# The gate and up projections of an FFN by seven block products in place of eight

## The chip, the cores and the metric

One core of a Trainium2 chip runs the whole program: one inference step of a model with two layers that share one code path. The metric is the device time of a launch in microseconds. Three runs of the kernel before gave a median of 1646.72 us (1646.56 to 1646.89).

## The reference

There are 640 tokens (512 of a sample, 128 of a prompt), a width of 1024 and two layers. Each layer has a token mixer and a gated FFN; the change lies in the FFN and in what surrounds it:

```
h = rms_norm(x, p["g_pre_ffn"]) * (1.0 + scale2) + shift2
f = (jax.nn.silu(h @ p["w_gate"]) * (h @ p["w_up"])) @ p["w_down"]
x = x + gate2 * rms_norm(f, p["g_post_ffn"])
```

h is 640 x 1024, w_gate and w_up are 1024 x 2816, w_down is 2816 x 1024, all in float32. The vectors scale2, shift2 and gate2, and three more for the mixer, come from a modulation: m = silu(cond) @ w_mod + b_mod, per layer, for two conditions.

## The kernel before

**Precision.** A float32 matrix product is made of three matmuls in the fp32r format. Each operand is split into hi (a rounded copy) and lo (what is left). `split` lets ScalarE write hi (L125) and VectorE or GpSimd write lo as source minus hi (L121); `mm3` issues hi*hi, hi*lo and lo*hi into one PSUM bank (L187 to L189).

**Weights.** `chunk` loads 512 KB by SP's DMA queue (L172) into a slot "raw" (three slots of 128 x 1024) and splits it into two pairs "wh", "wl" of 128 x 512 (eight slots each). In a gate or up chunk the eight k tiles of one f tile (128 of the 2816 columns) lie side by side.

**Input.** Normed tokens lie transposed in hTh and hTl: eight k tiles, 640 token columns, of which token tile t owns columns 128 t to 128 t + 127; tile 4 is the prompt. For each token tile the tail of the mixer makes the output projection, its post-norm (L382, L385), the statistic for the next norm (L344, with the root on POOL, L136), the normed rows (L352), their transposes on TensorE (L355), the modulation by scale and shift (L365 on ScalarE, L367 on VectorE), and a split into hTh and hTl. Tile 4 comes last.

**The FFN.** There are 22 f tiles in groups of 8, 8 and 6. For an f tile, gate and up are computed over two halves of the tokens, columns 0 to 255 (tiles 0 and 1) and 256 to 639: per half and matrix 8 k tiles times three matmuls. Then ScalarE takes tanh (L983), VectorE two steps that make silu(gate) * up (L984, L985), and a split makes hi and lo of the slot ft. In the first group the first four half products are of tiles 0 and 1 of f tiles 0 and 1, so that they need not wait for tiles 2 to 4. Behind each group stands its part of w_down, accumulated in SBUF (L1020, L1022). With the last group the post-norm follows, the residual rows xt are loaded, and in layer 0 the norm and transposes for layer 1.

**Background.** While the FFN of layer 0 runs, the modulation of layer 1 is computed by steps between f tiles: 512 KB of w_mod per DMA (L299) into slots of their own (tiles qa, kt and ka), multiplied by four matmuls side by side in the columns of TensorE (L302).

**Order.** The program is traced as one stream, and a scheduler places each engine's instructions in a queue; the engines then go through their queues in order and wait for each other on semaphores. Eight PSUM banks are in use: two tiles "s" of two banks, two "pt" of one, "o" and "g" of one.

## Time and profile before

| | value |
|---|---|
| median of three runs | 1646.72 us |
| span of the profiled execution | 1647.5 us |
| PE busy | 1588.7 us, 96% |
| PEld busy | 1362.7 us, 83% |
| DVE busy | 803.2 us, 49% |
| ACT busy | 662.9 us, 40% |
| POOL busy | 389.3 us, 24% |
| HBM read | 167.17 MB |

PE is TensorE's matmul pipe, PEld its weight loads, which run beside it; DVE is VectorE, ACT is ScalarE, POOL is GpSimd, SP issues the DMAs. Busy time is a sum over the span, so an engine that is busy for half of it may still be late in one stretch. The FFN of layer 0 lies between about 355 and 811 us and more, that of layer 1 from about 1163 us to the end. The page gives no time of the execution but its span, which is therefore the profiled execution's own time.

### The profile page before, as it was taken

The page shows a single profiled execution, that of the slowest core. Times are in us where ns is not written, and L with a number is a line of the kernel's source. Part 1 is how long each engine was busy: PE and PEld are TensorE (multiplying, and loading weights), DVE is VectorE, ACT ScalarE, POOL GpSimd, SP SyncE. Part 2 cuts the span into 40 slices and gives each one's busy share as a digit, 9 for nine tenths or more (in the row PEclk, how much of TensorE's full clock was granted, in tenths as well). Part 3 has the DMA queues.
Part 4 walks back from the last instruction along what each step waited for, and adds up shares of the span by engine and source line. Part 5 has one row for each costly group of instructions (what it writes and reads, how often), then busy time and mean ns, then how long its engine had stood idle before and what let it go on. Part 6 is the DMA issues. An engine that isn't in the chain of part 4 may idle for free.

```text
span 1647.5 us, 24545 instructions
## 1 busy us (share of the span) xinstructions
PE 1588.7 (96%) x9643; PEld 1362.7 (83%) x9643; DVE 803.2 (49%) x1553; ACT 662.9 (40%) x1472; POOL 389.3 (24%) x338
## 2 busy tenths in 40 slices
PE   7999989999999999999999999998899999999998
PEld 5676767678987989889978877776799889988996
DVE  4557777683231223332376687767723222333335
ACT  5343676563222322222254447765523222212222
POOL 3124214552100211021041242254511021101102
PEclk9999999999999999999999999999999999999999
DMA  9854020255453253122242111102422222213212
GB/s 327 307 179 162 29 84 27 78 185 203 165 205 115 90 192 125 56 97 77 71 164 91 55 61 55 39 26 103 167 90 77 71 84 77 68 49 102 77 65 77
DMA packets 62900, 180.08 MB, mean 109 GB/s; under 512 B 9520, under 2 KB 20784, under 8 KB 62784
## 3 DMA queue, kind: packets, MB, share of 16 engines
q1 hardware_dynamic: 62784, 178.50, 32.1%
q8 instruction: 76, 1.25, 0.3%
q14 instruction: 40, 0.33, 0.1%
HBM read 167.17 MB, written 11.30 MB: 108 GB/s over the span
## 4 chain that ended last, share of the span: by engine, by line
PE 83%; DVE 5%; issue 4%; ACT 4%; POOL 3%; DMA 1%; SPq 0%; DVEq 0%; POOLq 0%; ACTq 0%
PE s L187 8%; PE s L188 8%; PE s L189 8%; PE g L187 6%; PE g L189 6%; PE g L188 6%; PE o L187 5%; PE o L188 5%; PE o L189 5%; PE pt L187 5%; PE pt L188 4%; PE pt L189 4%; PE s L302 2%; PE o L602 2%; PE pt L593 2%
## 5 line engine op out<-in xcount | busy, mean ns | idle before, releaser
L121 DVE TENSOR_TENSOR wl<-raw,wh 128x512 fp32r<-128x512 f32 x240 | 189.0, 795 | 351.3 <-ACT wh L125 348.4
L125 ACT ACTIVATE wh<-raw 128x512 fp32r<-128x512 f32 x344 | 212.1, 631 | 342.9 <-PE s L188 153.6
L121 POOL TENSOR_TENSOR wl<-raw,wh 128x512 fp32r<-128x512 f32 x120 | 164.8, 1379 | 719.4 <-ACT wh L125 717.6
L187 PE MATMUL s<-hTh,wh 128*128 128x384 f32 (+1 forms) x928 | 290.0, 313 | 0.0
L188 PE MATMUL s<-hTl,wh 128*128 128x384 f32 (+1 forms) x928 | 289.0, 311 | 0.0
L189 PE MATMUL s<-hTh,wl 128*128 128x384 f32 (+1 forms) x928 | 288.3, 311 | 0.0
L187 PEld LDWEIGHTS s<-hTh,wh 128*128 128x128 f32 x928 | 174.4, 188 | 6.1 <-ACT P L983 4.2
L189 PEld LDWEIGHTS s<-hTh,wl 128*128 128x128 f32 x928 | 174.6, 188 | 0.0
L188 PEld LDWEIGHTS s<-hTl,wh 128*128 128x128 f32 x928 | 174.2, 188 | 0.2
L187 PE MATMUL pt<-hTh,wh 128*128 128x384 f32 (+1 forms) x448 | 140.1, 313 | 4.0 <-ACT hTh L125 3.9
L188 PE MATMUL pt<-hTl,wh 128*128 128x384 f32 (+1 forms) x448 | 139.6, 312 | 0.0
L189 PE MATMUL pt<-hTh,wl 128*128 128x384 f32 (+1 forms) x448 | 138.8, 310 | 0.0
L187 PE MATMUL g<-wh,hTh 128*128 128x512 f32 x256 | 106.5, 416 | 0.6 <-ACT hTh L125 0.5
L188 PE MATMUL g<-wl,hTh 128*128 128x512 f32 x256 | 103.8, 405 | 0.0
L189 PE MATMUL g<-wh,hTl 128*128 128x512 f32 x256 | 103.3, 404 | 0.4 <-DVE hTl L121 0.4
L136 POOL TENSOR_TENSOR rs<-rs,mhalf 128x1 f32<-128x1 f32 (+3 forms) x66 | 58.2, 885 | 176.8 <-DVE rs L133 126.9
L187 PEld LDWEIGHTS pt<-hTh,wh 128*128 128x128 f32 x448 | 84.5, 189 | 7.7 <-ACT hTh L125 5.1
L547 DVE TENSOR_REDUCE nm<-s 128x1 f32<-128x640 f32 x96 | 77.5, 820 | 27.0 <-PE s L546 13.9
L548 ACT ACTIVATE P<-s,nm 128x640 f32<-128x640 f32 x96 | 76.3, 797 | 28.8 <-DVE nm L547 27.4
L189 PEld LDWEIGHTS pt<-hTh,wl 128*128 128x128 f32 x448 | 84.8, 189 | 0.0
L188 PEld LDWEIGHTS pt<-hTl,wh 128*128 128x128 f32 x448 | 84.4, 188 | 0.3 <-DVE hTl L121 0.3
L984 DVE SCALAR_TENSOR_TENSOR P<-P,s 128x384 f32<-128x384 f32 (+1 forms) x58 | 28.2, 486 | 101.2 <-ACT P L983 101.2
(370 smaller groups left out, 3177.9 us busy)
## 6 DMA issues: line engine op xcount, KB each, us to landing
raw<-in_w_gate SPq DMA_DIRECT2D x44, 512.0 KB
raw<-in_w_up SPq DMA_DIRECT2D x44, 512.0 KB
raw<-in_w_down SPq DMA_DIRECT2D x44, 512.0 KB
kt<-in_w_mod SPq DMA_DIRECT2D x40, 512.0 KB
raw<-in_w_in SPq DMA_DIRECT2D x32, 512.0 KB
ka<-in_w_mod SPq DMA_DIRECT2D x24, 512.0 KB
raw<-in_w_out SPq DMA_DIRECT2D x16, 512.0 KB
qa<-in_w_mod SPq DMA_DIRECT2D x16, 512.0 KB
```

Of the source, the lines that this page charges most:

```text
L121: eng.tensor_tensor(lo, src, hi.bitcast(F32), op=ALU.subtract)
L125: self.S.activation(hi, src, AF.Copy)
L136: self.G.tensor_tensor(out, out, self.mhalf[:, :out.shape[-1]], op=ALU.pow)
L187: self.T.matmul(out, ah, bh, start=first, stop=False)
L188: self.T.matmul(out, ah, bl, start=False, stop=False)
L189: self.T.matmul(out, al, bh, start=False, stop=last)
L302: self.T.matmul(p[32 * j:32 * j + 32, 0:w], self.c2[:, c:c + 32], raw[k][j // 2][:, j % 2 * w:(j % 2 + 1) * w], start=c == 0, stop=c == 2 ...
L547: V.tensor_reduce(nm[:, s:s + 1], sc[:, :, :320], axis=AX.XY, op=ALU.max, negate=True)
L548: S.activation(P[s].rearrange("p (a b) -> p a b", a=2), sc[:, :, :320], AF.Exp, bias=nm[:, s:s + 1], accum_out=sm[:, s:s + 1])
L593: T.transpose(p[:, j - j0, i * 128:(i + 1) * 128], P[:, j * 128:(j + 1) * 128], self.ident)
L602: T.matmul(o[64 * i:64 * i + 64, 0:128], vt[:, j if nkt == 5 else 5], PT[:, j, i * 128:(i + 1) * 128], start=j == 0, stop=j == nkt - 1)
L984: V.scalar_tensor_tensor(ta, ta, 1.0, gp, op0=ALU.add, op1=ALU.mult)
```

## The change

The 640 x 1024 input is cut into 2 x 2 blocks: tokens 0 to 319 and 320 to 639 (so token tile 2 is cut in two), k tiles 0 to 3 and 4 to 7. The weights of a pair of f tiles are cut in the same way, 512 x 128 each. The eight block products of such a pair become seven, by Winograd's form of Strassen's algorithm: four input blocks enter as they are or combined with others, and so do the weight blocks; the results are formed by additions.

`combine` makes the combined inputs, 64 columns at a time, five times per layer, from the normed and modulated rows m in float32; those of columns c and c + 320 enter one call, so the first three calls need token tiles 2 and 3, the last two also tile 4. Products 6, 7 and 3 read new operands, product 5 reads a combination put in place into hTh and hTl, products 1, 2 and 4 read plain blocks. `wunit` makes four differences of a unit's weight blocks (a unit is gate or up of one pair, so there are 44 in all) and splits seven pieces. `fproduct` is one product, 12 matmuls of 320 columns; `funit` has the seven with five additions from PSUM on VectorE. For four units (the first two pairs) products 1 and 2 are placed early, between the combinations, and their weights are loaded a second time for the rest. Groups are now 2, 3, 3 and 3 pairs, the next group's first gate unit stands before w_down, the modulation of layer 1 goes through the "s" slots in 256 KB pieces (`mod_s`), and the last rows xt through "raw". In the trace of after, the split stands at L119, mm3 at L185, the products at L1035 to L1037, the combinations at L983 to L988, weight differences at L1014.

```diff
-HALVES = [(0, 256), (256, 384)]
-GROUPS = [list(range(0, 8)), list(range(8, 16)), list(range(16, 22))]
+HT = TOK // 2
+GROUPS = [[0, 1], [2, 3, 4], [5, 6, 7], [8, 9, 10]]
...
+    def mod_s(self, l, pair, p, bank):
+        src = self.a["w_mod"][l].rearrange("(k p) (i n) -> p k i n", p=128, n=D)
+        for k in range(KT):
+            for j in range(4):
+                raw = self.s()
+                self.SY.dma_start(raw, src[:, k, pair[j // 2], j % 2 * 512:(j % 2 + 1) * 512])
+                self.T.matmul(p[32 * j:32 * j + 32], self.c2[:, 2 * k:2 * k + 32], raw, start=k == 0, stop=k == KT - 1)
+            yield
+        self.mod_finish(l, pair, 512, 0, p, lambda what: self.s(), bank)
...
+        sl = slice(t * 128, min((t + 1) * 128, stop))
+        n = sl.stop - sl.start
+        if n > 0:
+            self.split(self.hTh[:, 4 * i:4 * i + 4, sl], self.hTl[:, 4 * i:4 * i + 4, sl], ht[:, :, 0:n], eng)
...
+    def operands(self):
+        s2, s3 = (self.tl(self.pa, [128, 2, 4, HT], "kt", 2, F32R) for _ in range(2))
+        s4 = [self.tl(self.pa, [128, 4, HT], "PT", 4, F32R) for _ in range(2)]
+        h, l = self.hTh, self.hTl
+        self.ops = {1: (h[:, 0:4, 0:HT], l[:, 0:4, 0:HT]), 2: (h[:, 4:8, 0:HT], l[:, 4:8, 0:HT]),
+                    4: (h[:, 4:8, HT:TOK], l[:, 4:8, HT:TOK]), 5: (h[:, 0:4, HT:TOK], l[:, 0:4, HT:TOK]),
+                    6: (s2[:, 0], s2[:, 1]), 7: (s3[:, 0], s3[:, 1]), 3: s4}
+    def combine(self, m, c):
+        V, G = self.V, self.G
+        def q(col, i):
+            return m[col // 128][i].rearrange("p (k n) -> p k n", n=128)[:, :, col % 128:col % 128 + 64]
+        a11, a12, a21, a22 = q(c, 0), q(c, 1), q(c + HT, 0), q(c + HT, 1)
+        w, x = (self.ptile()[:, 0:512].rearrange("p (a k n) -> p a k n", a=2, k=4) for _ in range(2))
+        out = lambda n: [x[:, :, c:c + 64] for x in self.ops[n]]
+        V.tensor_tensor(w[:, 0], a21, a22, op=ALU.add)
+        G.tensor_tensor(x[:, 0], a11, a21, op=ALU.subtract)
+        V.tensor_tensor(w[:, 1], w[:, 0], a11, op=ALU.subtract)
+        G.tensor_tensor(x[:, 1], a12, w[:, 1], op=ALU.subtract)
+        for n, y in ((6, w[:, 1]), (7, x[:, 0]), (5, w[:, 0]), (3, x[:, 1])):
+            self.split(*out(n), y, V)
...
+    def wunit(self, w, pair, tmp=None, early=False):
+        V, G = self.V, self.G
+        tmp = tmp or self.s
+        b11, b21 = self.wraw(w, 2 * pair)
+        d = {1: self.wpiece(b11, V), 2: self.wpiece(b21, G)}
+        if early:
+            yield d
+            b11, b21 = self.wraw(w, 2 * pair)
+        b12, b22 = self.wraw(w, 2 * pair + 1)
+        def diff(a, b, e):
+            o = tmp()
+            e.tensor_tensor(o, a, b, op=ALU.subtract)
+            return o
+        t1 = diff(b12, b11, V)
+        t2 = diff(b22, t1, V)
+        d[6] = self.wpiece(t2, V)
+        t3 = diff(b22, b12, G)
+        t4 = diff(b21, t2, G)
+        d[7] = self.wpiece(t3, V)
+        d[5] = self.wpiece(t1, V)
+        d[4] = self.wpiece(t4, G)
+        d[3] = self.wpiece(b22, V)
+        yield d
...
+        wh, wl = w[n]
+        for k in range(4):
+            c = slice(k * 128, (k + 1) * 128)
+            a, b = (wh[:, c], wl[:, c]), (ah[:, k, :], al[:, k, :])
+            o = bank[:, 0:HT]
+            self.T.matmul(o, a[0], b[0], start=first and k == 0, stop=False, skip_group_check=True)
+            self.T.matmul(o, a[0], b[1], start=False, stop=False, skip_group_check=True)
+            self.T.matmul(o, a[1], b[0], start=False, stop=last and k == 3, skip_group_check=True)
...
+    def funit_a(self, w, a):
+        g1 = self.ptile()
+        self.fproduct(w, 1, a, last=False)
+        self.S.activation(g1[:, 0:HT], a[:, 0:HT], AF.Copy)
+        yield g1
+        self.fproduct(w, 2, a, first=False)
+        yield g1
+    def funit(self, w, a, g1, bank, second=None):
+        V = self.V
+        n = slice(0, HT)
+        h = slice(HT, TOK)
+        g2, xu = self.ptile(), self.ptile()
+        b = bank()
+        self.fproduct(w, 6, b)
+        V.tensor_tensor(xu[:, n], b[:, n], g1[:, n], op=ALU.add)
+        bank(b)
+        if second:
+            next(second)
+        d = bank()
+        self.fproduct(w, 7, d)
+        V.tensor_tensor(xu[:, h], d[:, n], xu[:, n], op=ALU.add)
+        bank(d)
+        c = bank()
+        self.fproduct(w, 5, c, last=False)
+        V.tensor_tensor(g2[:, h], c[:, n], xu[:, h], op=ALU.add)
+        e = bank()
+        self.fproduct(w, 4, e)
+        V.tensor_tensor(g1[:, h], e[:, n], xu[:, h], op=ALU.add)
+        bank(e)
+        self.fproduct(w, 3, c, first=False)
+        V.tensor_tensor(g2[:, n], c[:, n], xu[:, n], op=ALU.add)
+        bank(c)
+        return a, g1[:, h], g2
...
-        big = [self.tl(pa, [128, 3, 1024], tag, n) for tag, n in (("kt", 2), ("kt", 2), ("ka", 1))]
-        acc = [big[1][:, 0], big[1][:, 1], big[1][:, 2], big[0][:, 0], big[0][:, 1]]
-        rows = [big[2][:, 0], big[2][:, 1]]
-        xs = [big[0][:, 2], big[2][:, 2]]
...
+        def mods(gi):
+            if l == 0 and gi:
+                yield from self.mod_s(1, ((1, 0), (4, 3), (2, 5))[gi - 1], self.pg(), self.pg)
...
+        for c in range(0, 192, 64):
+            self.combine(m, c)
+        for pair in GROUPS[0]:
+            for w in ("w_gate", "w_up"):
+                ops = self.wunit(a[w][l], pair, (lambda: next(tmp)) if pair == 0 else None, True)
+                p = two[pair][:, len(parts) % 2]
+                parts.append(self.funit_a(next(ops), p))
+                first[w, pair] = (ops, next(parts[-1]), p)
+            for x in parts[-2:]:
+                next(x)
+        for c in range(192, HT, 64):
+            self.combine(m, c)
+        held = gate(unit("w_gate", 0))
+        acc = [x[:, i] for tag, n in (("qa", 2), ("VB", 3))
+               for x in [self.tl(pa, [128, n, 1024], tag, 1)] for i in range(n)]
+        ka = self.tl(pa, [128, 2, 2, 640], "ka", 1, F32R)
+        slot = lambda tag, n: (lambda: self.tl(pa, [128, 2, 640], tag, n, F32R))
+        fts = self.ring([slot("t5", 3)] * 3 + [slot("PT", 4)] * 2 + [ka[:, 0], ka[:, 1]])
...
+            for pair in ps:
+                if pair != ps[0]:
+                    held = gate(unit("w_gate", pair))
+                self.step(bg, PACE, mark)
+                up(pair, unit("w_up", pair), *held)
+                self.step(bg, PACE, mark)
+            self.step(bg, 99, mark)
...
+                held = gate(unit("w_gate", GROUPS[gi + 1][0]))
             for n in range(2):
-                w = self.unit([a["w_down"][l, n, fp] for fp in range(fs[0] // 2, fs[-1] // 2 + 1)], self.es("wd"))
+                w = self.unit([a["w_down"][l, n, pair] for pair in ps], self.es("wd"))
...
-                            xt = xs[t % len(xs)]
+                            xt = self.tl(self.wp, [128, 1024], "raw", 3)
```

**The order at the head of layer 0's FFN, TensorE.** Here s_810 and pt are the transposes' banks, o the last of the output projection, s_851, s_835 and pt_3856 banks of FFN products, wh and wl weights, and kt the combined operand of product 6. Before, where the first products begin:

```order
L355 MATMUL s_810_3679<-identr_77,s_2500 128x128 x4
L189 MATMUL o_3803<-wh_3431,hTl_89 128x512
L187 MATMUL s_851_3884<-hTh_88,wh_3865 128x256
L188 MATMUL s_851_3884<-hTl_89,wh_3865 128x256
L189 MATMUL s_851_3884<-hTh_88,wl_3866 128x256
L187 MATMUL s_851_3884<-hTh_88,wh_3865 128x256
```

After, the end of a product 1, the transposes of token tile 4, and the start of a product 2:

```order
L1035 MATMUL s_835_3854<-hTh_88,wh_3931 128x320
L1036 MATMUL s_835_3854<-hTl_89,wh_3931 128x320
L1037 MATMUL s_835_3854<-hTh_88,wl_3932 128x320
L365 MATMUL pt_3832<-identr_77,t_477_2504 128x128 x4
L365 MATMUL pt_3833<-identr_77,t_477_2504 128x128 x4
L1035 MATMUL s_835_3854<-hTh_88,wh_3911 128x320
```

After, where the early products end and product 6 of the first unit begins:

```order
L1036 MATMUL s_836_3855<-hTl_89,wh_4007 128x320
L1037 MATMUL s_836_3855<-hTh_88,wl_4008 128x320
L1035 MATMUL pt_3856<-kt_3858,wh_4083 128x320
L1036 MATMUL pt_3856<-kt_3858,wh_4083 128x320
L1037 MATMUL pt_3856<-kt_3858,wl_4084 128x320
```

Before, products go on with the second half's operand of hTh. After, eight products of 320 columns stand ahead of product 6, and the transposes of tile 4 stand among them; what follows is queued behind product 6.

**The order there on VectorE.** Here hTl is the input's lo part, t_477 and s are work space, P a work tile, wl the lo of weights, VB a slot of weight differences. Before, up to the last split of the input:

```order
L984 SCALAR_TENSOR_TENSOR P_4010<-P_4010,g_3960 128x256
L121 TENSOR_TENSOR PT_3883<-P_3933,PT_3883 128x256
L367 TENSOR_SCALAR t_477_2504<-pt_3834,mc_93 128x128
L985 SCALAR_TENSOR_TENSOR P_4010<-P_4010,o_3961 128x256
L367 TENSOR_SCALAR t_477_2504<-pt_3835,mc_93 128x128
L367 TENSOR_SCALAR t_477_2504<-pt_3834,mc_93 128x128
L121 TENSOR_TENSOR PT_3959<-P_4010,PT_3959 128x256
L367 TENSOR_SCALAR t_477_2504<-pt_3835,mc_93 128x128
L121 TENSOR_TENSOR hTl_89<-t_477_2504,hTh_88 128x4x128
```

After, up to the last operand of product 6 (kt_3858):

```order
L119 TENSOR_TENSOR wl_4102<-raw_4079,wh_4101 128x512
L983 TENSOR_TENSOR P_4049<-t_477_2504 128x256
L983 TENSOR_TENSOR P_4063<-t_477_2504 128x256
L985 TENSOR_TENSOR P_4049<-P_4049,s_2498 128x256
L119 TENSOR_TENSOR wl_4190<-VB_3862,wh_4189 128x512
L985 TENSOR_TENSOR P_4063<-P_4063,s_2500 128x256
L119 TENSOR_TENSOR hTl_89<-P_4049,hTh_88 128x4x64
L119 TENSOR_TENSOR kt_3859<-P_4050,kt_3859 128x4x64
L119 TENSOR_TENSOR hTl_89<-P_4063,hTh_88 128x4x64
L119 TENSOR_TENSOR kt_3858<-P_4049,kt_3858 128x4x64
L1014 TENSOR_TENSOR s_4291<-raw_4289,raw_4287 128x512
L119 TENSOR_TENSOR kt_3858<-P_4063,kt_3858 128x4x64
```

The last split of tile 4 was followed by products; now the sums of `combine` (L983, L985), their lo parts and weight pieces stand between the modulation of tile 4 and product 6.

**VectorE in the steady part of layer 0.** In both, wl are the weights' lo, s a weight difference, P the work tile of silu. Before:

```order
L984 SCALAR_TENSOR_TENSOR P_6150<-P_6150,s_1110_6101 128x256
L985 SCALAR_TENSOR_TENSOR P_6150<-P_6150,s_1110_6101 128x256
L121 TENSOR_TENSOR t_1109_6100<-P_6150,t_1109_6100 128x256
L121 TENSOR_TENSOR wl_6366<-raw_6359,wh_6365 128x512
L984 SCALAR_TENSOR_TENSOR P_6206<-P_6206,pt_6156 128x384
L985 SCALAR_TENSOR_TENSOR P_6206<-P_6206,pt_6157 128x384
L121 TENSOR_TENSOR wl_6376<-raw_6369,wh_6375 128x512
L121 TENSOR_TENSOR t_1109_6100<-P_6206,t_1109_6100 128x384
```

After:

```order
L1057 TENSOR_TENSOR P_6117<-pt_3856,P_6102 128x320
L119 TENSOR_TENSOR wl_6231<-raw_6228,wh_6230 128x512
L1063 TENSOR_TENSOR P_6117<-pt_3857,P_6117 128x320
L1014 TENSOR_TENSOR s_6240<-raw_6238,raw_6228 128x512
L1014 TENSOR_TENSOR s_6242<-raw_6238,s_6240 128x512
L1067 TENSOR_TENSOR P_6116<-s_835_3854,P_6117 128x320
L119 TENSOR_TENSOR wl_6245<-s_6242,wh_6244 128x512
L119 TENSOR_TENSOR wl_6253<-s_6248,wh_6252 128x512
L119 TENSOR_TENSOR wl_6257<-s_6240,wh_6256 128x512
L119 TENSOR_TENSOR wl_6265<-raw_6238,wh_6264 128x512
L1070 TENSOR_TENSOR P_6102<-s_835_3854,P_6117 128x320
L119 TENSOR_TENSOR wl_6396<-raw_6393,wh_6395 128x512
```

An f tile had two steps per half and its weights; a unit now has differences, lo pieces and adds out of PSUM (L1057, L1063, L1067, L1070) in one queue.

## Rows read from the trace of the kernel before

**Rows 1.** The page: span, busy time of each engine, chain that ended last.

```profile
span 1647.5 us, 24545 instructions
...
PE 1588.7 (96%) x9643; PEld 1362.7 (83%) x9643; DVE 803.2 (49%) x1553; ACT 662.9 (40%) x1472; POOL 389.3 (24%) x338
...
PE 83%; DVE 5%; issue 4%; ACT 4%; POOL 3%; DMA 1%; SPq 0%; DVEq 0%; POOLq 0%; ACTq 0%
```

**Rows 2.** Windows: stretch, its us, each engine's busy us, PEclk, DMA share, GB/s.

```profile
351.60:373.00 21.40, 20.25 (x159) 17.20 (x157) 20.56 (x40) 15.02 (x36) 11.82 (x11) 1.00 0.79 273
374.00:487.00 113.00, 112.98 (x754) 103.83 (x754) 32.64 (x63) 32.19 (x60) 16.75 (x13) 1.00 0.54 188
725.60:811.00 85.40, 85.40 (x578) 85.40 (x577) 28.78 (x51) 24.98 (x47) 12.32 (x10) 1.00 0.29 94
1163.00:1184.00 21.00, 15.20 (x121) 14.61 (x120) 19.62 (x40) 14.29 (x34) 9.34 (x9) 0.96 0.75 252
1182.50:1185.90 3.40, 2.84 (x9) 2.84 (x10) 0.82 (x2) 1.02 (x2) 1.27 (x1) 0.50 0.02 5
1185.90:1189.00 3.10, 3.10 (x19) 3.10 (x18) 0.00 (x0) 0.64 (x1) 1.29 (x1) 1.00 0.00 0
```

**Rows 3.** Timeline of PE, products of 256 columns: start, us, instruction.

```profile
461.59 0.28 PE L188 MATMUL pt<-hTl,wh 128*128 128x256 f32 x1
461.71 0.28 PE L189 MATMUL pt<-hTh,wl 128*128 128x256 f32 x1
```

**Rows 4.** Tile raw, 550 to 660 us: min/median/max ns of its readers.

```profile
L125 ACT ACTIVATE wh<-raw x28: 622/633/634, 555.4 to 655.4; 128x512 fp32r<-128x512 f32 x28
L121 DVE TENSOR_TENSOR wl<-raw,wh x17: 692/693/1416, 549.8 to 656.1; 128x512 fp32r<-128x512 f32 x17
L121 POOL TENSOR_TENSOR wl<-raw,wh x13: 1284/1284/1292, 549.3 to 639.7; 128x512 fp32r<-128x512 f32 x13
```

**Rows 5.** DVE's groups by form, 374 to 640 us: busy, mean ns, idle before.

```profile
L984 DVE SCALAR_TENSOR_TENSOR P<-P,pt 128x384 f32<-128x384 f32 x5 | 2.7, 549 | 2.2 <-ACT P L983 2.2
```

**Rows 6.** Timeline of DVE (two rows) and POOL (last) from 543 us on.

```profile
543.70 1.25 DVE L121 TENSOR_TENSOR wl<-raw,wh 128x512 fp32r<-128x512 f32 x1 [21.79 <-ACT wh L125]
545.09 3.25 DVE L121 TENSOR_TENSOR wl<-raw,wh 128x512 fp32r<-128x512 f32 x2 [0.15 <-ACT wh L125]
...
543.09 4.71 POOL L121 TENSOR_TENSOR wl<-raw,wh 128x512 fp32r<-128x512 f32 x3 [88.39 <-ACT wh L125]
```

**Rows 7.** Timeline of DVE ahead of the FFN of layer 0.

```profile
350.55 0.68 DVE L382 TENSOR_TENSOR s<-s,ka 128x512 f32<-128x512 f32 x1
...
364.11 0.69 DVE L121 TENSOR_TENSOR hTl<-s,hTh 128x512 fp32r<-128x512 f32 x1
364.71 0.69 DVE L344 SCALAR_TENSOR_TENSOR t<-PT 128x512 f32<-128x512 f32 x1
...
370.51 0.42 DVE L121 TENSOR_TENSOR PT<-P,PT 128x256 fp32r<-128x256 f32 x1
370.85 0.41 DVE L367 TENSOR_SCALAR t<-pt,mc 128x128 f32<-128x128 f32 x1
371.17 0.41 DVE L985 SCALAR_TENSOR_TENSOR P<-P,o 128x256 f32<-128x256 f32 x1
```

**Rows 8.** Timeline of POOL, same place.

```profile
351.60 3.00 POOL L121 TENSOR_TENSOR wl<-raw,wh 128x512 fp32r<-128x512 f32 x2
```

**Rows 9.** Timeline of PE, same place: modulation, then the second half's products.

```profile
370.65 1.07 PE L302 MATMUL g<-qa,c 128*32 128x512 f32 x8
...
373.55 0.44 PE L187 MATMUL pt<-hTh,wh 128*128 128x384 f32 x1
```

**Rows 10.** Timeline of DVE, then of PE, ahead of the FFN of layer 1.

```profile
1159.84 1.77 DVE L385 SCALAR_TENSOR_TENSOR ka<-s,rs,ka 128x512 f32<-128x512 f32 x1 [0.43 <-POOL rs L136]
...
1183.06 1.01 PE L187 MATMUL pt<-hTh,wh 128*128 128x384 f32 x2 [3.87 <-ACT hTh L125]
```

114 lines of the change are left out of this document (62 added, 52 removed).

## The prediction

> **What bounds the kernel now.** I began with the page: its first rows give a span of 1647.5 us with TensorE busy in 96% of it and VectorE in 49%, and the chain that ended last is TensorE's for 83% [rows 1]. The reader is to see that TensorE's queue sets the time, so that removed matmuls count in full as long as nothing else becomes late. The windows over the FFN come next [rows 2]. Between 374 and 487 us, in layer 0 with the modulation's background work in it, PE is busy 112.98 of 113.00 us, and between 725.6 and 811 us all 85.40 us, six f tiles, at granted clock 1.00. Six f tiles are 576 matmuls of 256 or 384 columns (two products, two halves, eight k tiles, three terms each), so a mean 320-column matmul costs 85.40 / 576 = 0.148 us. A 256-column one costs 0.12 us from start to start [rows 3], with its own weight load beside it, so 320 columns leave room for the load. In that window DVE is busy a third (28.78 us) and POOL a seventh (12.32 us): there is cover to spend, but it isn't boundless.
>
> **What goes.** A unit is gate or up of a pair of f tiles: 96 matmuls before, 7 x 12 = 84 of 320 columns after. There are 44 units, so 528 matmuls go: 528 x 0.148 = **-78.2 us**. A unit falls from 14.2 to 84 x 0.148 = 12.4 us, one product is 1.78 us.
>
> **What comes in, in the steady part.** Per unit VectorE now has five lo pieces and two differences of 512 columns, five PSUM adds of 320, half a pair's tanh and gate steps, and one 640-wide lo. Two SBUF operands of 512 cost 0.60 us from start to start [rows 7]; an instruction with a PSUM operand costs 0.55 us at 384 columns [rows 5], taken as 0.40 us at 320 less the overlap of neighbours. That makes 7 x 0.60 + 5 x 0.40 + 1.6 + 0.7 = 8.5 us per unit, under 12.4. ScalarE has seven hi pieces of 0.63 us [rows 4], and a copy of 320, tanh and one hi of 640 each, which at the same speed per column make 2.0 us more, 6.4 in all; GpSimd has two differences and two lo pieces of 1.28 us [rows 4], 5.1 us. All three would hide under the matmuls, were they independent. They are not: where DVE and POOL split weights at the same time, a DVE piece took 1.25 us and two took 3.25 us, instead of 0.69 each, while POOL needed 4.71 us for three [rows 6]: 2.6 us of DVE's time went in waits beside three POOL instructions, 0.87 each. Over the head of the FFN the loss is smaller. Between 351.6 and 373 us DVE is busy 20.56 us for 40 instructions [rows 2]. By the starts of neighbours they need 0.60 us at 512 columns (17 of them), 0.34 at 256 (6) and 0.32 at 128 with two scalars (12) [rows 7], with 0.4 for five small ones 16.4 us. The other 4.2 us fall on seven POOL instructions with SBUF operands (its first two took 3.00 us, not 2.57 [rows 8]): 0.6 each.
>
> The Trainium skill, "SBUF — State Buffer", section "Who interferes with whom", says that a DVE instruction with two SBUF inputs contends with a GpSimd instruction that reads SBUF, under a lock that is held for the whole instruction, and that whoever issues first wins. The trace agrees in kind [rows 6], but its mean loss is half of a POOL instruction. By the whole-instruction price a unit would cost VectorE more than TensorE: that is the first rival's price.
>
> With 0.67 us (4 x 0.67 = 2.7) VectorE needs 11.2 us per unit, still under 12.4, but at 90% of it. What shows is lateness: product 3 accumulates in the bank of product 5, and VectorE must have read it first, with only product 4 (1.78 us) between. An add behind one lo piece and one POOL instruction takes 0.40 + 0.60 + 0.67 = 1.67 us and fits; behind a second lo it is 2.9 us, 1.2 late. At one unit in four that is 0.3 us per unit, **+11 us** for the 36 units after the first four of each layer; bounds 0 (hidden) and 36 x 1.16 = 42 (DVE blocked for the whole 1.28 us of each: 8.5 + 4 x 1.28 = 13.6 per unit).
>
> **The heads.** This is the largest debit. Before, products start with the first half of the tokens and go on with the second as soon as tile 4 is normalised: 96 half products' matmuls (11.5 us), 24 modulation matmuls from 370.65 to 373.55 us, then 384-column products without a stop [rows 2, 9]. After, only products 1 and 2 of four units (8 x 1.78 = 14.2 us) need the first half; product 6 and all later ones need the combined operands, whose last slices need tile 4. In the changed order the wait stands on product 6 in TensorE's queue, with everything of the FFN behind it. Its last operand is VectorE's 68th instruction after the first lo piece of the FFN: 25 of 512 columns, 28 of 256, 12 of 128 and three tiny ones, 15.0 + 9.5 + 3.8 + 0.4 = 28.7 us of its own; and 13 wide and 10 half-width POOL instructions stand beside it, 13 x 0.6 + 10 x 0.3 = 10.8 us. With 1.4 us for waits on the norm's roots, from 351.2 us (where L382, started at 350.55, lets go [rows 7]) this makes 392 us. By then the kernel before has done 11.5 + 2.9 + 18.5 = 32.9 us of work, after 14.2: 18.7 lost. In layer 1 the same stretch begins at about 1159.3 (its L385 starts at 1159.84 [rows 10]) and ends at 1200; before, the 384-column products began at 1183.06 [rows 10], at half clock for 3.4 us and then full [rows 2]: 11.5 + 1.7 + 14.1 = 27.3 against 14.2, 13.1 lost (less than in layer 0, since PE already stood still there: 15.20 of 21 us busy [rows 2]). The granted clock fell to 0.50 for 3.4 us after such an idle stretch [rows 2], which costs 1.7 us; four stretches where one was, 3 x 1.7 = 5. Together **+37 us**. Bounds: with no blocking and no half clock product 6 starts at 381 and 1189, which loses 6.6 and 1.5, 8 in all; with each POOL instruction blocking in full (13 x 1.28 + 10 x 0.66 = 23 us) it is 404 and 1212, 31 + 25 + 5 = 61. I take the middle, since the stretch before, with the same mixture, gave it.
>
> **The first four units** of each layer still find VectorE behind (their own differences were queued among the combinations): 0.5 us each, **+4** (2 to 10).
>
> **The modulation** of layer 1 loses its own slots. Its 256 KB raws now take the eight "s" slots that the differences use, one vector pair per group after the first, and stand ahead of weight loads in SP's queue; a wait for a slot there holds the next weights. Before, the same matmuls sat between products without a gap (374 to 487 us [rows 2]). 24 steps at a quarter microsecond are **+6** (0 to 24 x 1.78 = 43, one product lost per step).
>
> **Ends.** At each layer's last pair no next gate unit is held between the up unit and w_down, so add, tanh, gate and split stand open, about 2 us; a fourth group adds ten accumulations per layer, hidden; layer 1's w_in loads share the three raw slots with the FFN's last rows. **+6** (2 to 12).
>
> **Sum.** -78.2 + 37 + 4 + 11 + 6 + 6 = -14, against the profiled span of 1647.5: 1633.3. The median of the runs, 1646.72, lies 0.8 below that span, so **1632.5 us**.
>
> **Rivals.** First, the lock between DVE and POOL sets the pace of the steady units: 13.6 us each, +42 in place of +11, 1663.5, slower. It decides once a POOL instruction costs DVE over (12.4 - 8.5) / 4 = 0.98 us. For it: 0.87 measured where both had a queue [rows 6], and VectorE will have one all the time. Against: 0.6 over the head. Second, the overheads hide: heads at their low end with half-clock stretches (8 + 5), 2, 2, 3 and 4 for the rest, 24 in all, 1592.5. For it: DVE is a third busy now. Against: the head's own work alone outlasts the early products. Third, the modulation's raws hold SP's queue: +43 for +6, 1669.5, and only in layer 0; against it, eight slots are one and a half steps deep. That the change might not do what it says can be shut out by counting: 3696 matmuls of 320 columns stand where 4224 stood.
>
> **How the numbers follow.** Forecast 0.48, first rival 0.25, second 0.17, third 0.10. The likeliest case's own range is 1613 to 1650 (its heads and lateness half as large or half again). The range to hold 8 of 10 reaches into the first and second rival: 1600 to 1666. A measurement of this kernel tells 0.2% (3.3 us) from no change. Faster: 0.41 of the forecast, all of the second, 0.02 of the first: 0.60. The same: 0.05 + 0.02 + 0.01 = 0.08. Slower: 0.32.
>
> **What would show it.** Right: PE idle before the first product 6 until about 392 and 1200 us; DVE near 11 us of each 12.7 us unit in the middle of layer 1, PE there over 97%; wl pieces on DVE at a mean near 1 us. The heads are wrong if product 6 starts before 383 or after 403; the lock if a steady unit takes over 13.2 us; the modulation if layer 0's units are longer than layer 1's by over 0.5 us. Any PE stretch in which the granted clock stays at half beyond a start, or gaps that DMA ends, would make the prediction wrong by a cause that I have left out.

## The result and the profile after

The changed kernel took 1704.92 us (median of four runs, 1702.69 to 1709.17) against 1646.81 us: a ratio of 1.0354, with a 95% interval of 1.0339 to 1.0370. It is 58 us slower, where 14 us less had been forecast. The profiled execution has a span of 1700.9 us, 53.4 over the span of before [rows 1]; it was the fastest of the four runs. The shares below are of that span.

The page after: span, busy time of each engine, PE's busy tenths in 40 slices, and the chain that ended last.

```profile
span 1700.9 us, 24487 instructions
...
PE 1560.0 (92%) x9115; PEld 1303.3 (77%) x9115; DVE 1155.8 (68%) x1981; ACT 753.0 (44%) x1618; POOL 560.6 (33%) x446
...
PE   7999999968999999999988999998589999999897
...
PE 67%; DVE 17%; issue 5%; ACT 4%; DMA 3%; POOL 2%; SPq 0%; DVEq 0%; POOLq 0%; ACTq 0%
```

TensorE's work did fall, by 28.7 us of busy time even by this measure, in which clock and gaps mix. VectorE rose from 803.2 to 1155.8 us and GpSimd from 389.3 to 560.6, and in the chain that sets the end VectorE's share went from 5% to 17%. The two low slices, a 6 in the ninth and a 5 in the 29th, are the heads of the two FFNs.

The windows by stage: stretch, its length, busy us of each engine (with the number of instructions), PEclk, DMA share, GB/s. The first three are layer 0's head (from tile 3's post-norm to the first product 6), its first four units, and the rest of its gate and up; the next three are the same for layer 1; the last three are stretches at half clock.

```profile
353.10:394.80 41.70, 27.32 (x134) 24.15 (x132) 40.97 (x66) 25.01 (x60) 28.83 (x24) 0.80 0.31 114
394.80:448.00 53.20, 46.32 (x276) 44.28 (x277) 45.05 (x66) 20.41 (x36) 18.96 (x13) 0.90 0.35 115
448.00:827.00 379.00, 368.95 (x2098) 306.70 (x2097) 229.61 (x331) 127.65 (x222) 104.38 (x68) 1.00 0.39 132
1195.40:1239.30 43.90, 25.54 (x133) 23.07 (x132) 43.14 (x65) 26.18 (x63) 31.44 (x26) 0.77 0.31 108
1239.30:1291.30 52.00, 45.21 (x279) 43.58 (x278) 44.67 (x67) 19.78 (x35) 17.61 (x13) 0.93 0.23 78
1291.30:1640.00 348.70, 331.28 (x1917) 306.20 (x1916) 232.64 (x324) 128.79 (x221) 103.65 (x68) 0.98 0.22 77
1354.30:1357.60 3.30, 2.89 (x11) 2.89 (x12) 1.35 (x3) 0.00 (x0) 0.00 (x0) 0.50 0.45 159
1480.60:1484.00 3.40, 3.40 (x15) 3.40 (x14) 1.36 (x2) 1.10 (x2) 1.28 (x1) 0.51 0.28 113
1603.50:1610.30 6.80, 5.41 (x20) 5.41 (x21) 3.60 (x7) 1.76 (x4) 1.28 (x1) 0.50 0.23 77
```

Of the 41.7 and 43.9 us of the heads PE is busy for 27.3 and 25.5, at 0.80 and 0.77 of the clock. In the next two stretches 276 and 279 matmuls of 0.148 us (40.8 and 41.3 us) took 53.2 and 52.0 us, with VectorE busy for 45 of them. In the long stretches PE stands still for 10.0 and 17.4 us, and layer 1's mean clock of 0.98 means 14 of 348.7 us at half, 7 us lost. In the kernel before, the corresponding stretch of layer 0 had no gap [rows 2].

Who PE waited for from 350 us on: us in total, number of waits, the longest. The first three rows are of everything from there on, the next four of layer 0's long stretch, the last two of layer 1's.

```profile
PE s L1035 <- DVE P L1067: 20.3, 10, 4.0
PE s L1035 <- ACT P L1043: 14.2, 5, 7.7
PE pt L365 <- DVE s L362: 8.2, 2, 7.7
...
PE pt L1035 <- ACT wh L123: 5.0, 5, 2.2
PE s L1035 <- DVE P L1067: 2.5, 3, 1.6
PE s L1035 <- ACT wh L123: 1.3, 2, 0.7
PE pt L1037 <- DVE wl L119: 1.2, 3, 0.9
...
PE s L1035 <- DVE P L1067: 13.7, 5, 4.0
PE s L1035 <- ACT wh L123: 3.4, 5, 0.7
```

L1067 is the add that reads product 5's bank, L1043 ScalarE's copy that reads product 1's bank. The five waits for L1043 all lie in the heads (375 to 391 and 1227 to 1236 us). In the long stretches PE waits for L1067, 16.2 us in all, and for the hi and lo pieces of weights (L123, L119), 10.9 us. One of the waits for L1067, VectorE's timeline first (start, us, instruction, idle before it):

```profile
1349.94 1.91 DVE L1116 SCALAR_TENSOR_TENSOR P<-P,P 128x640 f32<-128x640 f32 x1
1352.65 1.01 DVE L119 TENSOR_TENSOR ka<-P,ka 128x640 fp32r<-128x640 f32 x1 [0.80 <-ACT ka L123]
1353.58 0.68 DVE L119 TENSOR_TENSOR wl<-raw,wh 128x512 fp32r<-128x512 f32 x1
1354.18 0.48 DVE L1067 TENSOR_TENSOR P<-s,P 128x320 f32<-128x320 f32 x1
...
1378.00 0.81 DVE L1116 SCALAR_TENSOR_TENSOR P<-P,P 128x640 f32<-128x640 f32 x1
```

GpSimd at the same time:

```profile
1349.55 1.62 POOL L1014 TENSOR_TENSOR s<-raw,s 128x512 f32<-128x512 f32 x1 [1.68 <-PE pt L1037]
1351.13 1.85 POOL L119 TENSOR_TENSOR wl<-s,wh 128x512 fp32r<-128x512 f32 x1
```

And TensorE, the first and the last matmul of product 5, the first of product 4 and the first of product 3:

```profile
1349.14 0.31 PE L1035 MATMUL s<-hTh,wh 128*128 128x320 f32 x1
...
1350.76 0.31 PE L1037 MATMUL s<-hTh,wl 128*128 128x320 f32 x1
1354.71 0.64 PE L1035 MATMUL s<-hTh,wh 128*128 128x320 f32 x1 [3.65 <-DVE P L1067]
...
1359.65 0.31 PE L1035 MATMUL s<-PT,wh 128*128 128x320 f32 x1
```

Product 5 ended just after 1350.8. The add (L1067) that had to read it started at 1354.18, behind a gating step that took 1.91 us beside two GpSimd instructions (the same step takes 0.81 at 1378.00), a wait for ScalarE, a 640-wide lo and a weight's lo. TensorE stood for 3.65 us and came back at half clock.

The matmul that waited is of product 4: it reads hTh, whereas product 3, which goes on in product 5's bank, reads PT and starts at 1359.65 without a wait. All ten waits for L1067 end with a matmul on hTh. Products 5 and 4 have banks of their own, but these are the two halves of one tile "s" (in the order ahead of the prediction L1067 and L1070, which read them, both name s_835), and the program makes product 4 wait for the read of the other half: its first matmul waits for L1067 in 40 of the 44 units, product 3's in two.

Over layer 1's long stretch VectorE is 67% busy, but w_down lies in it too. Two units that follow each other took 28.0 us in place of 2 x 12.4:

```profile
1362.20:1390.20 28.00, 25.42 (x168) 24.66 (x168) 23.97 (x33) 12.29 (x22) 12.83 (x8) 1.00 0.21 76
```

There VectorE is busy for 12.0 us per unit, 86%. It is nearly full, but its work, blocked time included, would still fit under the 12.4 us of TensorE; it is late at the place that counts.

### The profile page after: what moved, and what is told of

It reads as the page before. It is cut to its first block, busy times and chain, and to the rows that moved or that the text cites. A ratio compares the mean times of both kernels' runs of the same rounds, so it can differ in the third digit from the quotient of the medians.

```text
span 1700.9 us, 24487 instructions
## 1 busy us (share of the span) xinstructions
PE 1560.0 (92%) x9115; PEld 1303.3 (77%) x9115; DVE 1155.8 (68%) x1981; ACT 753.0 (44%) x1618; POOL 560.6 (33%) x446
## 4 chain that ended last, share of the span: by engine, by line
PE 67%; DVE 17%; issue 5%; ACT 4%; DMA 3%; POOL 2%; SPq 0%; DVEq 0%; POOLq 0%; ACTq 0%
PE s L1035 6%; PE g L185 6%; PE g L187 6%; PE g L186 6%; PE s L1036 6%; PE s L1037 5%; PE o L185 5%; PE o L186 5%; PE o L187 4%; DVE wl L119 4%; PE pt L1037 2%; PE pt L1035 2%; DVE s L1014 2%; PE pt L1036 2%; PE g L287 2%
## 5 line engine op out<-in xcount | busy, mean ns | idle before, releaser
L123 ACT ACTIVATE wh<-raw 128x512 fp32r<-128x512 f32 x300 | 183.2, 628 | 257.8 <-PE s L1036 130.0
L1035 PE MATMUL s<-hTh,wh 128*128 128x320 f32 x680 | 221.8, 326 | 43.3 <-DVE P L1067 20.3
L119 DVE TENSOR_TENSOR wl<-raw,wh 128x512 fp32r<-128x512 f32 x240 | 200.9, 844 | 45.5 <-ACT wh L123 42.5
L1036 PE MATMUL s<-hTl,wh 128*128 128x320 f32 x680 | 216.9, 319 | 0.6 <-DVE hTl L119 0.6
L1037 PE MATMUL s<-hTh,wl 128*128 128x320 f32 x680 | 216.3, 318 | 0.0
L119 POOL TENSOR_TENSOR wl<-raw,wh 128x512 fp32r<-128x512 f32 x76 | 112.7, 1489 | 276.1 <-ACT wh L123 168.9
L1035 PEld LDWEIGHTS s<-hTh,wh 128*128 128x128 f32 x680 | 133.6, 196 | 63.4 <-DVE P L1067 22.9
L123 ACT ACTIVATE wh<-s 128x512 fp32r<-128x512 f32 x160 | 98.4, 630 | 182.9 <-PE s L1036 83.6
L1037 PEld LDWEIGHTS s<-hTh,wl 128*128 128x128 f32 x680 | 133.8, 197 | 3.9 <-DVE wl L119 1.7
L1014 POOL TENSOR_TENSOR s<-raw 128x512 f32<-128x512 f32 x40 | 65.5, 1638 | 198.6 <-PE g L287 91.4
L1035 PE MATMUL pt<-kt,wh 128*128 128x320 f32 x352 | 112.0, 318 | 5.9 <-ACT wh L123 5.0
L1036 PE MATMUL pt<-kt,wh 128*128 128x320 f32 x352 | 111.3, 316 | 6.2 <-DVE kt L119 6.2
L119 DVE TENSOR_TENSOR wl<-s,wh 128x512 fp32r<-128x512 f32 x120 | 103.5, 874 | 19.8 <-ACT wh L123 18.1
L1037 PE MATMUL pt<-kt,wl 128*128 128x320 f32 x352 | 111.5, 318 | 1.2 <-DVE wl L119 1.2
L185 PE MATMUL g<-wh,hTh 128*128 128x512 f32 x256 | 105.6, 412 | 0.5 <-ACT hTh L123 0.5
L560 DVE TENSOR_REDUCE nm<-s 128x1 f32<-128x640 f32 x96 | 77.3, 819 | 26.2 <-PE s L559 13.1
L119 POOL TENSOR_TENSOR wl<-s,wh 128x512 fp32r<-128x512 f32 x40 | 61.0, 1525 | 89.2 <-ACT wh L123 89.1
```

What stands on the lines that cost most here:

```text
L119: eng.tensor_tensor(lo, src, hi.bitcast(F32), op=ALU.subtract)
L123: self.S.activation(hi, src, AF.Copy)
L185: self.T.matmul(out, ah, bh, start=first, stop=False)
L560: V.tensor_reduce(nm[:, s:s + 1], sc[:, :, :320], axis=AX.XY, op=ALU.max, negate=True)
L1014: e.tensor_tensor(o, a, b, op=ALU.subtract)
L1035: self.T.matmul(o, a[0], b[0], start=first and k == 0, stop=False, skip_group_check=True)
```

## The experiments

All ratios are to the kernel before, run on the same chip, with 95% intervals; its median lay between 1646.8 and 1648.8 us there, so a difference between two runs below is uncertain by some 2 us. "Head", "first units" and "units" are stretches as in the windows above.

**Product 3 in a bank of its own** (its output is incomplete: product 5's share in one quarter is left out).

```diff
         V.tensor_tensor(g2[:, h], c[:, n], xu[:, h], op=ALU.add)
+        bank(c)
...
-        self.fproduct(w, 3, c, first=False)
-        V.tensor_tensor(g2[:, n], c[:, n], xu[:, n], op=ALU.add)
-        bank(c)
+        f = bank()
+        self.fproduct(w, 3, f)
+        V.tensor_tensor(g2[:, n], f[:, n], xu[:, n], op=ALU.add)
+        bank(f)
```

> Product 3 gets a PSUM bank of its own, so it no longer waits for VectorE's read of product 5's bank; the addition of product 5's result in that quarter of the output is left out, all else stands. Theory (the place decides): the waits of product 3 for that add (20.3 us over the span in the changed kernel) and the half-clock stretches behind them (about 8 us) go, the time falls by 20 to 30 us, to about 1680. Rival (VectorE's throughput decides, wherever it is read): the wait moves to the next add, bank or weight piece, and the time falls by 8 us at most.

Measured: 1692.48 us, ratio 1.0266 (1.0251 to 1.0281), 12 us less. PE's waits, as above:

```profile
PE s L1035 <- ACT P L1043: 15.0, 8, 4.4
PE s L1035 <- DVE P L1057: 11.4, 8, 3.2
...
PE s L1035 <- DVE P L1063: 6.9, 4, 2.3
```

The wait for L1067 is gone, but 18 us of waits for two other adds (L1057, product 6's bank, and L1063, product 7's) have come up in its place: half of the theory and half of the rival. The edit does more than its name says. Banks are handed out in turn, and with one more taken per unit all products change banks, so other products now share a tile. The run shows that the waits move with the banks; that product 3's own wait was the cause it can't show, for in the changed kernel the wait stood on product 4.

**Product 5 first, copied by ScalarE** (nothing left out; the pieces of its weights are made first, too). VectorE has as many instructions as in the changed kernel.

```diff
+        d[5] = self.wpiece(t1, V)
         t2 = diff(b22, t1, V)
...
-        d[5] = self.wpiece(t1, V)
...
+        c = bank()
+        self.fproduct(w, 5, c, last=False)
+        self.S.activation(g2[:, h], c[:, n], AF.Copy)
         b = bank()
         self.fproduct(w, 6, b)
...
-        c = bank()
-        self.fproduct(w, 5, c, last=False)
-        V.tensor_tensor(g2[:, h], c[:, n], xu[:, h], op=ALU.add)
+        V.tensor_tensor(g2[:, h], g2[:, h], xu[:, h], op=ALU.add)
```

> Product 5 is moved ahead of product 6 and ScalarE copies its result at once, so that product 3 can go on in its bank without waiting for VectorE, which adds the copy later; nothing is left out. Theory (product 3 waits behind VectorE's queue): as much comes back as with the bank of its own (12.4 us), or a little more: 1688 to 1693. Rival (the wait passes to the next read that VectorE makes): under 5 us.

Measured: 1678.87 us, ratio 1.0189 (1.0171 to 1.0207), 26 us less, more than expected. PE's waits:

```profile
PE s L1035 <- ACT P L1043: 16.8, 5, 7.1
...
PE s L1035 <- DVE P L1110: 6.8, 5, 2.0
```

The largest wait for VectorE is now 6.8 us in total (L1110, the gating step, which frees the bank of products 1 and 2). With the same number of adds and weight pieces on VectorE, 26 us came back by giving one read to another engine: order, and not the amount of VectorE's work alone, made these units slow. Here, too, the banks change hands (product 5 holds its bank longer), so which part of the gain is the read's and which the new sharing of tiles isn't shown.

**GpSimd out of the weights.** Three runs belong together: all gate and up weights on VectorE; the same with 176 GpSimd instructions beside it whose result nobody uses; the same with 176 that only write.

```diff
-        d = {1: self.wpiece(b11, V), 2: self.wpiece(b21, G)}
+        d = {1: self.wpiece(b11, V), 2: self.wpiece(b21, V)}
...
-        t3 = diff(b22, b12, G)
-        t4 = diff(b21, t2, G)
+        t3 = diff(b22, b12, V)
+        t4 = diff(b21, t2, V)
...
-        d[4] = self.wpiece(t4, G)
+        d[4] = self.wpiece(t4, V)
```

> All differences and lo pieces of the gate and up weights are made by VectorE, none by GpSimd. Theory of the lock: a GpSimd instruction beside a busy VectorE costs it about 1 us, more than the 0.6 us of doing the work itself, so the time falls by 10 to 30 us. Rival (VectorE's own work decides, the lock costs 0.6 us or less): each unit gives VectorE 2.4 us more of its own against 4 x 0.6 saved, and the time stays within 5 us or rises by up to 20.

Measured: 1673.24 us, ratio 1.0150 (1.0135 to 1.0165), 32 us less. PE's waits for L1067 fell from 20.3 us to about half:

```profile
PE s L1035 <- DVE P L1067: 10.6, 7, 2.0
```

The two edits beside it, each switched on for four pieces of every unit:

```diff
         self.split(h, l, src, eng)
+        if beside:
+            d = self.tl(self.wp, [128, 512], "dm", 1, mybir.dt.bfloat16)
+            self.G.tensor_tensor(d, h.bitcast(F32), src, op=ALU.subtract)
```

> The version with gate and up weights on VectorE alone (1673), and beside it four GpSimd instructions per unit that read a weight's hi and source and write a scratch tile that nobody uses: 176 as in the changed kernel, but none that anyone waits for. Theory (GpSimd's reads block VectorE): 20 to 35 us are lost again, 1693 to 1708. Rival (in the changed kernel the pieces that GpSimd makes come late, VectorE isn't disturbed): within 5 us of 1673.

Measured: 1765.59 us, ratio 1.0720 (1.0701 to 1.0738), 92 us more than without them, over two and a half times the upper end of what the theory had expected. These instructions also hold the slots that they read, which would be another cause, but the only other engine that waited for them was ScalarE, for 4.6 us in all. PE's waits for product 5's add (here L1070) rose from 10.6 to 34.4 us:

```profile
PE s L1038 <- DVE P L1070: 34.4, 11, 5.0
```

```diff
+        if beside:
+            self.G.memset(l.bitcast(F32), 0.0)
         self.split(h, l, src, eng)
```

> As the run with GpSimd beside VectorE, but its four instructions per unit only write: each fills the lo slot with zeros before VectorE writes it, and reads nothing from SBUF. Theory (what blocks VectorE is GpSimd's reading): within 6 us of 1673, VectorE's busy time near the 1144 us of the version on VectorE alone, not 1298. Rival (any GpSimd instruction there disturbs VectorE, or the loss came from the extra waits on a second engine): 15 us or more above 1673.

Measured: 1672.31 us, ratio 1.0151 (1.0131 to 1.0171), no change. The page's row of busy times for the three, in that order:

```profile
PE 1549.8 (93%) x9115; PEld 1296.6 (78%) x9115; DVE 1143.9 (68%) x2157; ACT 754.8 (45%) x1618; POOL 297.3 (18%) x270
```

```profile
PE 1577.6 (89%) x9115; PEld 1315.0 (74%) x9115; DVE 1297.7 (73%) x2157; ACT 752.7 (43%) x1618; POOL 573.0 (32%) x446
```

```profile
PE 1552.4 (93%) x9115; PEld 1297.6 (78%) x9115; DVE 1147.0 (69%) x2157; ACT 755.6 (45%) x1618; POOL 385.6 (23%) x446
```

And GpSimd's added group in the last two (line, engine, operation, count | busy, mean ns | idle before):

```profile
L996 POOL TENSOR_TENSOR dm<-wh,raw 128x512 bf16<-128x512 f32 x88 | 139.4, 1584 | 315.3 <-ACT wh L123 220.9 <-DVE P L1073 53.0 <-issue 20.7
```

```profile
L994 POOL MEMSET wl<- 128x512 f32 x176 | 92.4, 526 | 715.8 <-PE s L1039 290.2 <-PE o L186 152.4 <-PE g L186 140.1
```

With the same VectorE instructions, 176 GpSimd instructions that read SBUF add 1297.7 - 1143.9 = 153.8 us to VectorE's busy time, 0.87 us each; 176 that write only add 3.1. The block comes from reading, and it works both ways: GpSimd's subtraction (into bf16) took 1.58 us instead of the 1.28 of before [rows 4]. The writes are shorter (0.53 us each, 92.4 us in all, where the three reading groups had 278.5), so this pair doesn't hold the duration equal, but a loss in proportion would still be 51 us of VectorE's busy time. In the changed kernel the price was 0.67: moving its 176 instructions gave VectorE 176 x 0.60 = 106 us of work, and its busy time fell by 12.

**Modulation matmuls side by side.**

```diff
-            for j in range(4):
-                raw = self.s()
-                self.SY.dma_start(raw, src[:, k, pair[j // 2], j % 2 * 512:(j % 2 + 1) * 512])
-                self.T.matmul(p[32 * j:32 * j + 32], self.c2[:, 2 * k:2 * k + 32], raw, start=k == 0, stop=k == KT - 1)
+            raw = [self.s() for _ in range(4)]
+            for j in range(4):
+                self.SY.dma_start(raw[j], src[:, k, pair[j // 2], j % 2 * 512:(j % 2 + 1) * 512])
+            for j in (3, 2, 1, 0):
+                self.T.matmul(p[32 * j:32 * j + 32], self.c2[:, 2 * k:2 * k + 32], raw[j], start=k == 0, stop=k == KT - 1)
```

> The four modulation matmuls of a step are issued behind their four DMAs with the last-loaded one first, so that they stand together in TensorE's queue (groups of 4 and 8 in place of 30 groups, 16 of them of one). Theory: a lone one takes 0.98 us, as four side by side do; the 192 records took 39.5 us against 22.6 before, and 12 to 16 us come back: about 1691. Rival: those matmuls stood where TensorE would have waited for VectorE anyway, and under 4 us come back; second rival: four slots at once hold the differences up, and it is slower.

Measured: 1692.82 us, ratio 1.0267 (1.0249 to 1.0284), 12 us less. What the theory rests on, in TensorE's timeline of the changed kernel: one modulation matmul (two records) between two products.

```profile
507.05 0.31 PE L1037 MATMUL s<-hTh,wl 128*128 128x320 f32 x1
507.28 1.05 PE L287 MATMUL g<-s,c 128*32 128x512 f32 x2
508.26 0.42 PE L1035 MATMUL pt<-kt,wh 128*128 128x320 f32 x1
```

From 507.28 to 508.26 TensorE does one of the four matmuls of a step, and needs about the 1.07 us in which the kernel before did four, eight records [rows 9]. Summed over layer 0 the groups take 39.5 us, 33.8 with this edit (21 groups in place of 30) and 22.6 before. These sums run to the start of the next matmul. Without the waits that lie in them (2.3 us, and 10.3 with this edit) the groups take 37.2 and 23.5 us: 14 us came back in the matmuls, but 8 us of new waits, for product 5's add, stand right behind three of them. So a net 6 of the 12 us are seen there; the rest I could not place.

**No combinations** (products 3, 5, 6 and 7 read plain blocks, so the FFN's result is another).

> No input combinations are made: products 3, 5, 6 and 7 read plain blocks of the input (their sums are left out), with all weight differences, matmuls and adds unchanged. Theory: the head of each FFN, lost for want of the combined operands, comes back (39 us counted from the landmarks) with a part of the 23 us of the first four units: 40 to 55 us, about 1655. Rival: the head is held by the weights' differences and lo pieces in VectorE's queue, not by the combinations: 10 to 20 us come back.

```diff
-                    6: (s2[:, 0], s2[:, 1]), 7: (s3[:, 0], s3[:, 1]), 3: s4}
+                    6: (h[:, 0:4, 0:HT], l[:, 0:4, 0:HT]), 7: (h[:, 4:8, 0:HT], l[:, 4:8, 0:HT]),
+                    3: (h[:, 4:8, HT:TOK], l[:, 4:8, HT:TOK])}
...
-        for c in range(0, 192, 64):
-            self.combine(m, c)
...
-        for c in range(192, HT, 64):
-            self.combine(m, c)
```

Measured: 1679.12 us, ratio 1.0180 (1.0165 to 1.0195), 26 us less. The first product 6 of layer 0, in TensorE's timeline:

```profile
379.89 0.41 PE L1036 MATMUL pt<-hTh,wh 128*128 128x320 f32 x1 [1.72 <-ACT t L375]
```

From tile 3's post-norm (351.2) that is 28.7 us instead of 41.7, and 31.6 instead of 43.9 in layer 1: 25 us, all of the gain. So the combinations, with the wait for tile 4 that they bring to product 6, are 25 of the heads' loss; what the rest is no run separates (the late norm of tile 4 and the weight pieces are my guess). The first four units were no shorter (61.7 and 60.6 us from product 6 to the first w_down eviction, 62.3 and 61.0 in the changed kernel), so their loss isn't the combinations'.

**Residual rows out of the weight slots.**

```diff
-                            xt = self.tl(self.wp, [128, 1024], "raw", 3)
+                            xt = xs[t]
```

> The residual rows of the FFN's tail go into the freed operand slots (tile kt) and no longer share the three weight slots with layer 1's first weights. Theory: the stretch from the last w_down accumulation of layer 0 to the first softmax of layer 1, 137.4 us in the changed kernel against 130.2 before, falls back, and the time by 5 to 8 us. Rival: that stretch is longer for another reason (the weights of the last units and w_down come late to the slots), and the time stays within 2 us.

Measured: 1698.32 us, ratio 1.0305 (1.0286 to 1.0323): a few us less, but the stretch that the theory named didn't change (137.8 us after 137.4). The theory fell; where the few us come from stays open.

**The four edits together** (GpSimd out of the weights, product 5 copied early, modulation side by side, rows in kt).

> Four edits together: differences and lo pieces of gate and up on VectorE alone, modulation matmuls side by side, product 5 copied early by ScalarE, residual rows in kt. If the four costs are separate, the sum of their gains comes back (32 + 12 + 12 + 6 = 62 us: 1643). If lateness of VectorE's queue is one cost that several of them touch, about two thirds (40 to 45 us: 1660 to 1665). What then remains over the kernel before is the head and the first four units of each layer.

Measured: 1643.95 us, ratio 0.9976 (0.9962 to 0.9991). The gains added up for the most part (61 us of 76 by the single runs), and the seven products are just ahead of the eight.

**Plain products first.** Four f tiles per layer as before, with the combinations made beside them, all on VectorE; the other 36 units by seven products.

```diff
+        for f, hf in ((0, 0), (1, 0), (0, 1), (1, 1)):
+            product(f, hf)
         for c in range(0, 192, 64):
-            self.combine(m, c)
+            self.combine(m, c, 0)
+        product(2, 0)
+        product(2, 1)
...
+        for c in range(0, HT, 64):
+            self.combine(m, c, 1)
```

> The four edits, and the first four f tiles of each layer by plain half products as in the kernel before, while VectorE makes the combined operands beside them (product 5's in place, once the plain products have read the input); the other 36 units by seven products. Theory (the head and the first units cost 39 + 23 us because all products wait for the combinations and VectorE): 45 to 55 us less than with the four edits alone, at the price of 8 x 1.78 = 14 us of matmuls: about 1610, under the kernel before. Rival (VectorE's load moves the wait into the first units behind the plain ones): 1635 to 1650.

Measured: 1661.57 us, ratio 1.0088 (1.0069 to 1.0107), slower than the four edits alone, and outside what either theory had expected. PE's longest wait between the layers:

```profile
PE s L366 <- DVE qa L363: 12.7, 1, 12.7
```

The FFN itself was faster (498.6 us from tile 3's post-norm to layer 0's last accumulation, 505.6 with the four edits), but the stretch to layer 1's first softmax took 154.1 us instead of 136.8, and the end behind layer 1's last accumulation 21.4 instead of 9.3. Another order of slots had left the gate rows of the last post-norm without a free one until w_down was over. The next two runs test that, on this version and on the four edits:

```diff
-                rows = [self.row(l, 5, c, self.tl(pa, [128, 1024], "t5", 3)) for c in range(2)]
+                rows = [self.row(l, 5, c, self.tl(pa, [128, 1024], "PT", 4)) for c in range(2)]
```

> The version with plain products for the first four f tiles, with one edit more: the gate rows of the last post-norm go into freed PT slots instead of t5 slots. Theory: in that version all t5 slots hold operands of the last w_down, so the rows are loaded after it; the stretch from layer 0's last accumulation to layer 1's first softmax (154.1 us against 136.8 with the four edits alone) and the end after layer 1's last accumulation (21.4 us against 9.3) come back: 25 to 32 us, about 1632. Rival (plain products first move the wait elsewhere, the rows are no cause): within 5 us of 1662.

Measured: **1631.05 us, ratio 0.9901 (0.9884 to 0.9918)**. The two stretches fell to 138.1 and 7.0 us.

> The four edits together, with the gate rows in freed PT slots. There only the second row, for token tile 4, shares a slot with the last w_down's operands: theory 3 to 8 us back (two tails), about 1638. Rival: the tail waits for its own arithmetic, no change within 2 us. With the version above this tells whether the plain start or the seven products from the first unit on is better once the tail is the same.

Measured: 1640.84 us, ratio 0.9965 (0.9953 to 0.9977). The stretch between the layers stayed at 136.8, the end fell from 9.3 to 7.0 us.

So plain products first are worth 10 us with the same tail, and that version is 1% faster than the kernel before. Its page and three windows (layer 0's head with its plain products, layer 0's and layer 1's units):

```profile
span 1628.8 us, 24493 instructions
...
PE 1534.9 (94%) x9211; PEld 1296.5 (80%) x9211; DVE 1089.2 (67%) x2095; ACT 751.0 (46%) x1638; POOL 291.9 (18%) x266
...
PE   7999989989999999999998999898799999999998
```

```profile
351.30:412.00 60.70, 53.55 (x350) 52.05 (x350) 41.73 (x88) 30.52 (x69) 18.54 (x15) 0.94 0.32 105
448.00:820.00 372.00, 356.53 (x2112) 305.05 (x2111) 230.02 (x404) 133.99 (x239) 0.00 (x0) 1.00 0.43 145
1249.40:1600.00 350.60, 343.93 (x2001) 315.63 (x2001) 237.99 (x408) 140.62 (x253) 5.13 (x4) 1.00 0.27 88
```

The head is now busy for 53.6 of 60.7 us, and in layer 1's units PE stands still for 6.7 us, against 17.4. In layer 0's units, with the modulation among them, it stands for 15.5 us, more than the 10.0 of the changed kernel; the largest row of waits there is 2.7 us for the modulation's own loads, and no run says more.

## Why the prediction was wrong

**Right: the matmuls.** 528 fewer, at 0.147 us from start to start in the trace after (product 5 above: eleven steps from 1349.14 to 1350.76), as before. The 78 us were there to be had.

**Right in size: the heads.** Product 6 started at 394.8 us (392 forecast) and 43.9 us after tile 3's post-norm in layer 1 (40 forecast). By the forecast's own way of counting the work of before, 20.2 and 17 to 19 us were lost, 37 to 39 in all for the +37. Without the combinations 25 of them come back. The last operand came later than forecast, though: after its first matmuls product 6 stood for 3.0 us more in layer 0 and 3.2 in layer 1 for lo parts of the combination, until 400.7 us in layer 0; that is counted with the first units below. (The low bound of 8 is a slip: product 6 at 381 and 1189 takes 11 us off both 18.7 and 13.1, which leaves 10.)

**Right in the mean, wrong in the use: the lock.** The forecast took 0.67 us of VectorE per GpSimd instruction; the run that moved them gave 0.67, the run that only added them 0.87. The first rival asked for 0.98 to decide and priced 13.6 us per unit; the units took 12.4 + 34 / 36 = 13.3 in the mean and 14.0 where two follow each other, so by the forecast's own sign (over 13.2 us) the rival's size came true. Its mechanism did not: VectorE was busy for 12.0 us per unit there, more than the 11.2 forecast, but under TensorE's 12.4.

**The step that failed: lateness.** "At one unit in four that is 0.3 us per unit" was to price the reads that hold a bank: one lo piece and one GpSimd instruction ahead of the add would fit into product 4's 1.78 us. Neither the cover nor the queue was like that. The wait stood one product earlier than the forecast had it, on product 4, whose bank is the other half of product 5's tile, so product 4 gave no cover. Ahead of the add stood several instructions, two of them blocked, and a wait for ScalarE between. And in or behind the three longest of layer 1's five stops (2.94, 3.65 and 4.00 us) TensorE ran at half clock, 13.6 us in all (the last three windows), which the forecast had not counted; behind the other two (1.58 and 1.55 us) it did not. The term of 11 us was 34: 16.2 of waits for L1067, 10.9 of waits for pieces of weights, which the term had at nothing, 0.3 for product 6's add, and 7.0 of half clock. The same in the first four units, taken as +4 "0.5 us each": 12.4 + 10.7 = 23, of which PE stood still for 14 and the rest is mostly half clock (0.90 and 0.93 in the windows). The two runs that leave VectorE's work as large or larger and change what stands in front of what (product 5's copy) or who blocks whom (GpSimd out) gave 26 and 32 us back. What a tile of its own for product 4 would have given no run shows.

**Mis-sized: the modulation.** +6 was for slots and SP's queue. It was 37.2 - 22.6 = 15 (without the wait of 2.3 us, which is in the 34), by a mechanism that was not thought of: loads of single slots let the scheduler scatter four matmuls that used to share TensorE's columns, and a lone one takes as long as four. The third rival's place was right, its cause wasn't.

**Mis-sized: the ends.** +6 was about 10: 7 between the layers (137.4 us for 130.2) and 3 at the end (10.0 us for 7.1). The cause between the layers is open: neither rows in kt nor gate rows in PT shortened it in the versions with the seven products from the start.

In sum: 38 + 23 + 34 + 15 + 10 = 120, and 1.4 us already lost ahead of the first head, less 78 are +43 of the +53.4 measured. 10 us are not placed; some records of matmuls can be missing, and the stretches' borders are not sharp.

The two costs of lateness, in the long stretches and in the first units, were not independent guesses: both took an average over a queue where the price was set by what stood in it at one moment. The rule of the Trainium skill ("SBUF — State Buffer", "Who interferes with whom") holds here in both halves: a GpSimd instruction that reads SBUF blocks VectorE instructions with two SBUF inputs, one that only writes doesn't (1765.59 and 1672.31 against 1673.24 us). Its whole-instruction price is an upper bound of the mean: 0.67 and 0.87 of 1.28 us.

## What to carry to other kernels

When a change trades TensorE's work for work on the engines that feed it, look not at their busy share but at each read that frees a bank: count what stands ahead of it in its engine's queue, with its blocked duration, and compare that with the product that covers it. Look up in the trace which product waits: here two banks in one tile moved the wait forward by one product and took the cover away. Give such a read to an engine that is idle, or put products between, before anything else is saved. Start the new scheme only once its operands are ready, with the old one as cover, and check after a change of slots who was left without one.
